# The start byte of the matmuls' moving rows: a 272-column pitch, and one that keeps every row at byte 64 of a 256-byte block

## The chip, the cores and the metric

The kernel runs on one core of a Trainium2 chip. The metric is the device time of one execution in microseconds. Names of engines: PE is TensorE, PEld its weight loads, DVE is VectorE, ACT is ScalarE, POOL is GpSimd, SP issues DMAs.

## The reference, cut to what matters

Two layers over 16 meta tokens and 256 frames (272 positions, D_MODEL 1024, D_FF 2816), all float32. Layer 0 mixes with differential attention, layer 1 with sparse attention (DSA); each layer has a feed-forward block before and after its mixer:

```python
def _swiglu(x, wi, wo):
    a, b = jnp.split(x @ wi, 2, axis=-1)
    return (jax.nn.silu(a) * b) @ wo
...
    for layer in range(DEPTH):
        h = h + 0.5 * _swiglu(_rms_norm(h, ln_ffn1[layer]), ffn1_wi[layer], ffn1_wo[layer])
        hn = _rms_norm(h, ln_mix[layer])
        ...
        h = h + mix @ w_out[layer]
        h = h + 0.5 * _swiglu(_rms_norm(h, ln_ffn2[layer]), ffn2_wi[layer], ffn2_wo[layer])
    return h[:, N_META:]
```

So there are four feed-forward blocks (FFN 1 to 4 here, the four calls of `ffn` in the code).

## The kernel before, in words

Activations lie transposed: features on the 128 partitions, positions along a row. `h` holds 8 rows (KT = 8 blocks of 128 features) of T = 272 positions. A float32 product is made of float32r parts: every operand x is split into a high part (a float32r copy) and a low part (x minus it), and `mm3` issues three matmuls for one 128x128 block of weights: high weights by high activations (L246), high weights by low activations (L247), low weights by high activations (L248). The weights are the stationary operand, and each matmul has a weight load of its own; the activations are the moving operand, streamed a row of 272 (or 256) columns at a time from the partition.

The moving rows that this document is about:

- `X["h"]` and `X["l"]`, the norms' input, split (`xh`, `xl`; 8 rows each). `prep_x` writes them after every residual add, ACT the high part and DVE the low one. They feed the first half of every FFN (the "wi" half), the attention projections and the DSA projections. For FFN 4 they lie in the tile `W` (`x2`) and are read from column 16 on, since the meta tokens are no longer needed: 256 columns.
- `ah` and `al`, the feed-forward activations, split (FT = 22 rows each), written in `evac` and `act_lo`, read in the second half of an FFN (the "wo" half).

A wi half runs over 22 weight tiles (j); in each, over k = 0 to 7, and at each k three matmuls into `pa` and three into `pb`, all six from row k of `xh` and `xl`: 48 matmuls a tile, 1,056 in all. A wo half runs over 8 output blocks, each of two weight tiles of 11 rows: 33 matmuls a tile, 528 in all. A differential attention projection takes the same 8 rows for one output after another: three matmuls at each k, 24 an output, 72 a head (queries, keys, values; 8 heads). In DSA, `cqh` and `cql` (2 rows of 256 columns each) are the moving rows of the projection `q_abs`.

Weights come by DMA from SP's queue ahead of their use (`Stream.dma`), ACT makes the high part (L116), DVE the low part (L133). All engines run their instructions in the order in which the program is written; tiles of the pools `const`, `act` and `ev` get fixed addresses, in the order of their first use.

A row of 272 float32 columns is 1088 bytes, which is 4 x 256 + 64. So where one row starts at byte 0 of a 256-byte block of its partition, the next starts at byte 64, then 128, 192, and 0 again. By the addresses in the built program:

| moving rows | first byte of the tile | row pitch, bytes | byte of rows 0, 1, 2, 3 in a 256-byte block |
|---|---|---|---|
| `xh`, `xl` (FFN 1 to 3, projections) | 27136, 35840 | 1088 | 0, 64, 128, 192 (both tiles) |
| `ah`, `al` of FFN 1 | 152512, 176448 | 1088 | 192, 0, 64, 128 and 64, 128, 192, 0 |
| `ah`, `al` of FFN 2 and 3 | 148224, 172160 | 1088 | 0, 64, 128, 192 and 128, 192, 0, 64 |
| `x2` of FFN 4, from column 16 on | 46720 | 1088 | 192, 0, 64, 128 (both parts) |
| `ah`, `al` of FFN 4, from column 16 on | 148224, 172160 | 1088 | 64, 128, 192, 0 and 192, 0, 64, 128 |
| `cqh`, `cql` | 177536, 179584 | 1024 | 128 in every row |

All weight tiles (`wh`, `wl`) start at byte 128 of such a block, and a 128-column block of weights is 512 bytes, so every weight load starts at byte 128.

The three matmuls, and the write of the split rows:

```python
        PE.matmul(ps, wh, bh, start=start, stop=False)
        PE.matmul(ps, wh, bl, start=False, stop=False)
        PE.matmul(ps, wl, bh, start=False, stop=stop)
...
        ACT.activation(xh[:, k, c], h[:, k, c], AF.Copy, scale=g(k))
        DVE.scalar_tensor_tensor(xl[:, k, c], h[:, k, c], g(k), xh.bitcast(F32)[:, k, c],
```

Of the kernel before, what the change touches and what calls it, by code (L numbers as in the profile page):

```python
# [61 lines left out]
def trunk(ctx, tc, d, out):  # L62
    nc = tc.nc
    PE, ACT, DVE, POOL = nc.tensor, nc.scalar, nc.vector, nc.gpsimd

    const = ctx.enter_context(tc.tile_pool(name="const", bufs=1))
# [6 lines left out]
    ps = ctx.enter_context(tc.tile_pool(name="ps", bufs=1, space=PSUM))  # L73

    def psa():
        return ps.tile([128, 512], F32, name="pa", bufs=3)

    def psb():
        return ps.tile([128, 512], F32, name="pb", bufs=3)

    def psc():
        return ps.tile([128, 512], F32, name="pc", bufs=2)
# [87 lines left out]
    h = const.tile([128, KT, T], F32, name="h")  # L170
# [28 lines left out]
    def ln(i):  # L199
        return lambda k: gn[:, 8 * i + k:8 * i + k + 1]  # L200

    X = dict(h=const.tile([128, KT, T], F32R, name="xh"), l=const.tile([128, KT, T], F32R, name="xl"))
    acc = const.tile([128, T], F32, name="acc")
    R = const.tile([128, T], F32, name="R")

# [3 lines left out]

    def prep_x(k, g, c0=0):  # L210
        c = slice(c0, T)
        xh, xl = X["h"], X["l"]
        ACT.activation(xh[:, k, c], h[:, k, c], AF.Copy, scale=g(k))
        DVE.scalar_tensor_tensor(xl[:, k, c], h[:, k, c], g(k), xh.bitcast(F32)[:, k, c],  # L214
                                 op0=OP.mult, op1=OP.subtract)

    def prep_s(k, c0=0):
# [20 lines left out]
    def rstd(psum_tile, c0=0):  # L238
        c = slice(c0, T)
        PE.matmul(psum_tile[:, c], ones_d, acc[:, c], start=True, stop=True)  # L240
        load = log_exp_tables()
        t = small.tile([128, T], F32, name="sq")
        rsqrt(R[:, c], psum_tile[:, c], t[:, c], load)

    def mm3(ps, wh, wl, bh, bl, start, stop):
# [6 lines left out]
    for k in range(KT):  # L252
        c = slice(256 * k, 256 * k + 256)
        prep_x(k, ln(0))
        ACT.copy(wh0[:, c], r0[:, c])  # L255
        DVE.tensor_tensor(wl0[:, c], r0[:, c], wh0.bitcast(F32)[:, c], OP.subtract)
# [9 lines left out]
    W = const.tile([128, 16, T], F32, name="W")  # L266
# [13 lines left out]
    def evac_h(mt, ps, half, g, c0):  # L280
        c = slice(c0, T)
        if half:
            DVE.scalar_tensor_tensor(h[:, mt, c], ps[:, c], 0.5, h[:, mt, c], op0=OP.mult, op1=OP.add)
        else:
            DVE.tensor_tensor(h[:, mt, c], ps[:, c], h[:, mt, c], OP.add)
        if g is None:
            nc.sync.dma_start(out[:, mt, :], h[:, mt, c])
        else:
            prep_x(mt, g, c0)
            prep_s(mt, c0)  # L290

    def ffn(g_next, c0=0, extra=None, first=0):
        c = slice(c0, T)
        with tc.tile_pool(name="act", bufs=1) as actp, tc.tile_pool(name="ev", bufs=2) as ev:
            ah = actp.tile([128, FT, T], F32R, name="ah")
            al = actp.tile([128, FT, T], F32R, name="al")
            ub = {}

            def act_lo(j):
                DVE.tensor_tensor(al[:, j, c], ub.pop(j)[:, c], ah.bitcast(F32)[:, j, c], OP.subtract)  # L300

            def evac(j, pa, pb):
                t = ev.tile([128, T], F32, name="t")
                s = ev.tile([128, T], F32, name="s")
                b = ev.tile([128, T], F32, name="b")
                DVE.tensor_tensor(t[:, c], pa[:, c], R[:, c], OP.mult)  # L306
                last_silu.append(ACT.activation(s[:, c], t[:, c], AF.Silu))
                DVE.tensor_tensor(b[:, c], pb[:, c], R[:, c], OP.mult)
                ws.ahead()
                if j:  # L310
                    act_lo(j - 1)
                DVE.tensor_tensor(b[:, c], s[:, c], b[:, c], OP.mult)  # L312
                ACT.copy(ah[:, j, c], b[:, c])  # L313
                ub[j] = b

            pairs = {}
            for j in range(FT):
                wh, wl = ws.next()
                pa, pb = psa(), psb()
                for k in range(KT):  # L320
                    for m, ps in ((0, pa), (1, pb)):
                        s = slice((2 * k + m) * 128, (2 * k + m + 1) * 128)
                        mm3(ps[:, c], wh[:, s], wl[:, s], X["h"][:, k, c], X["l"][:, k, c],
                            k == 0, k == KT - 1)
                pairs[j] = pa, pb
                if j == first:
                    rstd(psc(), c0)
                    if extra:
                        extra(psc())
                if j >= first:  # L330
                    for i in sorted(pairs):
                        evac(i, *pairs.pop(i))
            act_lo(FT - 1)

            for mt in range(KT):
                ps = psc()
                for half in range(2):
                    wh, wl = ws.next()
                    for kk in range(11):
                        f = half * 11 + kk  # L340
                        s = slice(kk * 128, kk * 128 + 128)
                        mm3(ps[:, c], wh[:, s], wl[:, s], ah[:, f, c], al[:, f, c], f == 0, f == FT - 1)
                    if half == 0:
                        ws.ahead()
                evac_h(mt, ps, True, g_next, c0)
                ws.ahead()

    def diff_attention():
        with tc.tile_pool(name="da", bufs=2) as da, tc.tile_pool(name="dp", bufs=1) as dp:
# [11 lines left out]
            for i in range(2):  # L361
                p = dp.tile([128, 400], F32, name=f"pta{i}")
# [19 lines left out]
            def proj_qk(i):  # L382
                wh, wl = ws.next()
                ps = (psc(), psc()) if i == 1 else (pj(), pj())
                for m in range(2):
                    for k in range(KT):
                        s = slice((2 * k + m) * 128, (2 * k + m + 1) * 128)
                        mm3(ps[m][:, :T], wh[:, s], wl[:, s], X["h"][:, k, :], X["l"][:, k, :], k == 0, k == KT - 1)
                    if i == 0 and m == 0:
                        rstd(ps1())  # L390
                st[i] = dict(ps=ps)
# [21 lines left out]
            def proj_v(i):  # L413
                wh, wl = ws.next()
                ps = pj()
                for k in range(KT):
                    s = slice(k * 128, k * 128 + 128)
                    mm3(ps[:, :T], wh[:, s], wl[:, s], X["h"][:, k, :], X["l"][:, k, :], k == 0, k == KT - 1)
                v = da.tile([128, T], F32, name="v")
                DVE.tensor_tensor(v, ps[:, :T], R, OP.mult)  # L420
                st[i]["v"] = v
# [32 lines left out]
            def logits(i):  # L454
# [29 lines left out]
                for m in range(2):  # L484
                    DVE.tensor_tensor(mt[:, m, :], ps[m][0:16, 416:432], W[0:16, m * AH + i, 144:160], OP.add)
                DVE.tensor_reduce(out=ms[:, 0:2], in_=mt, axis=AX.X, op=OP.max)
                DVE.tensor_tensor(mt, mt, ms[:, 0:2].unsqueeze(2).to_broadcast([16, 2, NM]), OP.subtract)
                ACT.activation(mt, mt, AF.Exp)

            def soft_fin(i):  # L490
# [93 lines left out]
            n = AH  # L584
# [7 lines left out]
            g = [pj(), pj(), None, None]  # L592
# [31 lines left out]
    def dsa():  # L624
        q0 = NM
        Q = slice(q0, T)
        with tc.tile_pool(name="sa", bufs=2) as sa, tc.tile_pool(name="sp", bufs=1) as sp, \
# [16 lines left out]
            def ps1():  # L644
                turn[0] ^= 1
                return (psa, psb)[turn[0]]()
# [58 lines left out]
            for m in range(4):  # L705
                ps = ps1()
                for k in range(2):
                    s = slice((2 * m + k) * 128, (2 * m + k + 1) * 128)
# [202 lines left out]
            n = BH  # L911
            for i in range(n):
# [14 lines left out]
                    soft_fin(i - 1)  # L927
                if i >= 3:
                    av(i - 3)
            x2 = const.tile([128, 16, T], F32R, name="W")  # L930
            X["h"], X["l"] = x2[:, 0:KT, :], x2[:, KT:16, :]

            def wout_part(ps, w, m, k0, k1):
                wh, wl = w
# [6 lines left out]
            g = [psc(), None, None, None]  # L941
# [20 lines left out]
            for grp in (2, 3):  # L962
                w = ws.next()
                for m in range(2):
                    ps = psc()
# [1 line left out]
                    evac_h(2 * grp + m, ps, False, ln(5), q0)  # L967
                ws.ahead()

    ffn(ln(1), extra=build_bias, first=1)  # L970
    diff_attention()
    once.close()
    ffn(ln(3))
    ffn(ln(4))
    dsa()
    ffn(None, c0=NM)


def _layout(inp):
# [49 lines left out]
    oh = np.zeros((32, 400), f)  # L1029
    for j in range(NREL):  # L1030
        rel = j - 271
# [22 lines left out]
```

## Time and profile before

| | |
|---|---|
| time, median of 3 runs | 1081.26 us (1081.1 to 1084.32) |
| span of the profiled execution, first to last instruction | 1079.7 us, 1.6 below the median |
| PE busy | 1067.9 us, 99% of the span |
| weight loads busy (they overlap the matmuls) | 1021.7 us, 95% |
| DVE busy | 689.6 us, 64% |
| ACT busy | 542.7 us, 50% |
| DMA queue of the weights | 46.0% of 16 engines' span |

A matmul's duration in the trace is some 280 to 290 ns, more than twice the distance from one start to the next, because matmuls are pipelined. So busy time is no measure of what one costs; the distance between starts is. It is read from the timeline, whose starts have two decimals (10 ns), by dividing a stretch by the number of matmuls in it.

### The profile page before, as it was taken

What the parts mean: (1) busy time and instruction counts of PE and PEld (TensorE: products, weight loads), DVE (VectorE), ACT (ScalarE), POOL (GpSimd) and SP (SyncE); (2) the same over time, 40 slices, a digit from 0 to 9 for tenths busy, and PEclk for the clock granted to TensorE, in tenths of its full rate; (3) what the DMA queues carried; (4) which work ended last, traced back from release to release, by engine and by line L of the source; (5) the groups of instructions that cost most, each with busy time, mean ns of one, the idle gap of its engine ahead of it and who ended that gap; (6) DMA issues with size and microseconds to landing.
All of it is one profiled execution on the core that took longest, in us unless ns stands there. A gap on an engine that the chain in (4) does not pass through costs nothing.

```text
span 1079.7 us, 20010 instructions
## 1 busy us (share of the span) xinstructions
PE 1067.9 (99%) x8332; PEld 1021.7 (95%) x8332; DVE 689.6 (64%) x1191; ACT 542.7 (50%) x876; POOL 77.2 (7%) x111
## 2 busy tenths in 40 slices
PE   8999999999999999999999999999999999999998
PEld 7999999998889999999999999999876799999998
DVE  6567645577777666655576666546898657666542
ACT  6455444356687544444454444535856545444331
POOL 1200000042210000000000000000153100000000
PEclk9999999999999999999999999999999999999999
DMA  8985445533343454445654544455422025554461
GB/s 295 210 233 204 151 154 169 190 134 128 128 153 117 166 187 168 172 129 170 213 204 164 188 161 142 161 172 201 156 91 90 1 101 181 189 195 171 147 200 68
DMA packets 30809, 174.20 MB, mean 161 GB/s; under 512 B 3664, under 2 KB 5216, under 8 KB 16896
## 3 DMA queue, kind: packets, MB, share of 16 engines
q1 hardware_dynamic: 29808, 169.99, 46.0%
q0 software_dynamic: 912, 2.95, 1.5%
q8 instruction: 65, 1.06, 0.4%
q14 instruction: 24, 0.20, 0.1%
HBM read 171.47 MB, written 1.46 MB: 160 GB/s over the span
## 4 chain that ended last, share of the span: by engine, by line
PE 92%; DMA 2%; DVE 2%; ACT 1%; issue 1%; POOL 0%; SPq 0%; DVEq 0%; POOLq 0%; ACTq 0%
PE pa L246 11%; PE pa L247 11%; PE pa L248 11%; PE pc L246 9%; PE pc L247 9%; PE pc L248 9%; PE pb L247 8%; PE pb L246 8%; PE pb L248 8%; DMA wr<-w_ffn_wi 2%; PE pc L858 1%; PE pc L861 1%; DVE wl L133 1%; DMA h<-hT 1%; DVE sel L794 1%
## 5 line engine op out<-in xcount | busy, mean ns | idle before, releaser
L116 ACT CAST wh<-wr 128x2048 fp32r<-128x2048 f32 (+3 forms) x180 | 301.0, 1673 | 347.5 <-PE pb L247 176.0
L133 DVE TENSOR_TENSOR wl<-wr,wh 128x2048 fp32r<-128x2048 f32 (+3 forms) x188 | 368.0, 1958 | 48.6 <-PE pc L248 29.4
L246 PE MATMUL pa<-xh,wh 128*128 128x272 f32 (+1 forms) x736 | 213.0, 290 | 2.4 <-ACT wh L255 2.4
L248 PE MATMUL pa<-xh,wl 128*128 128x272 f32 (+1 forms) x736 | 212.7, 289 | 1.5 <-DVE wl L133 1.5
L247 PE MATMUL pa<-xl,wh 128*128 128x272 f32 (+1 forms) x736 | 213.1, 290 | 0.0
L246 PE MATMUL pc<-ah,wh 128*128 128x272 f32 (+1 forms) x704 | 201.6, 286 | 0.0
L247 PE MATMUL pc<-al,wh 128*128 128x272 f32 (+1 forms) x704 | 201.2, 286 | 0.0
L248 PE MATMUL pc<-ah,wl 128*128 128x272 f32 (+1 forms) x704 | 200.9, 285 | 0.0
L247 PE MATMUL pb<-xl,wh 128*128 128x272 f32 (+1 forms) x544 | 157.4, 289 | 0.0
L248 PE MATMUL pb<-xh,wl 128*128 128x272 f32 (+1 forms) x544 | 156.8, 288 | 0.0
L246 PE MATMUL pb<-xh,wh 128*128 128x272 f32 (+1 forms) x544 | 156.0, 287 | 0.0
L246 PEld LDWEIGHTS pa<-xh,wh 128*128 128x128 f32 x736 | 139.0, 189 | 7.3 <-ACT wh L255 3.7
L248 PEld LDWEIGHTS pa<-xh,wl 128*128 128x128 f32 x736 | 138.6, 188 | 2.0 <-DVE wl L133 1.7
L247 PEld LDWEIGHTS pa<-xl,wh 128*128 128x128 f32 x736 | 138.5, 188 | 0.2
L247 PEld LDWEIGHTS pc<-al,wh 128*128 128x128 f32 x704 | 132.6, 188 | 0.0
L248 PEld LDWEIGHTS pc<-ah,wl 128*128 128x128 f32 x704 | 132.5, 188 | 0.0
L246 PEld LDWEIGHTS pc<-ah,wh 128*128 128x128 f32 x704 | 132.3, 188 | 0.0
L306 DVE TENSOR_TENSOR t<-pa,R 128x272 f32<-128x272 f32 (+1 forms) x88 | 38.4, 436 | 117.0 <-PE pa L248 116.6
L246 PEld LDWEIGHTS pb<-xh,wh 128*128 128x128 f32 x544 | 103.1, 189 | 0.0
L247 PEld LDWEIGHTS pb<-xl,wh 128*128 128x128 f32 x544 | 102.5, 188 | 0.2 <-DVE xl L214 0.2
L248 PEld LDWEIGHTS pb<-xh,wl 128*128 128x128 f32 x544 | 102.4, 188 | 0.0
L313 ACT CAST ah<-b 128x272 fp32r<-128x272 f32 (+1 forms) x88 | 36.6, 416 | 75.1 <-DVE b L312 75.1
(326 smaller groups left out, 1723.9 us busy)
## 6 DMA issues: line engine op xcount, KB each, us to landing
wr<-w_ffn_wi SPq DMA_DIRECT2D x85, 1024.0 KB, 4.8
wr<-w_ffn_wo SPq DMA_DIRECT2D x64, 704.0 KB, 4.1
wr<-w_qk SPq DMA_DIRECT2D x8, 1024.0 KB, 4.7
wr<-w_out SPq DMA_DIRECT2D x8, 1024.0 KB, 4.9
wr<-w_v SPq DMA_DIRECT2D x8, 512.0 KB, 3.3
wr<-w_uqa SPq DMA_DIRECT2D x4, 1024.0 KB, 4.8
W<-fd POOLq DMA_DIRECT2D x8, 272.0 KB, 18.9
wr<-w_ffn_wi SPq DMA_DIRECT2D x7, 256.0 KB, 6.5
```

The costliest lines, as they stand in the source:

```text
L116: ACT.copy(w[:, c], self.raw[i][:, c])
L133: DVE.tensor_tensor(w[:, c], r[:, c], self.h[i].bitcast(F32)[:, c], OP.subtract)
L246: PE.matmul(ps, wh, bh, start=start, stop=False)
L247: PE.matmul(ps, wh, bl, start=False, stop=False)
L248: PE.matmul(ps, wl, bh, start=False, stop=stop)
L306: DVE.tensor_tensor(t[:, c], pa[:, c], R[:, c], OP.mult)
L313: ACT.copy(ah[:, j, c], b[:, c])
L794: DVE.scalar_tensor_tensor(sel[:, b, kc], r[:, kc], wt[:, b, 2 * i + e:2 * i + e + 1], sel[:, b, kc], op0=OP.mult, op1=OP.add)
L858: PE.matmul(ps[:, B1], qas[i][:, 256 * k + 128:256 * k + 256], ckg[:, k, :], start=k == 0, stop=k == 1)
L861: PE.matmul(ps[:, B0], qas[i][:, 256 * k:256 * k + 128], ckg[:, k, 0:144], start=k == 0, stop=k == 1)
```

## The change

The rows get a pitch of a whole number of 256-byte blocks, and padding ahead of the tiles puts the first one at byte 64. `xh` and `xl` get rows of 320 columns (1280 bytes, XS), `ah` and `al` rows of 320 columns in FFN 1 to 3 and of 256 in FFN 4 (AS). In FFN 4 the activations are written from column 0 of their rows, no longer from column 16, and so is `x2`, which becomes 17 x 256 columns, addressed 48 columns in. The columns that are computed are the same.

```diff
+XS = 320
+AS = (320, 320, 320, 256)
...
-    X = dict(h=const.tile([128, KT, T], F32R, name="xh"), l=const.tile([128, KT, T], F32R, name="xl"))
+    const.tile([128, 16], F32, name="pad0")
+    X = dict(h=const.tile([128, KT, XS], F32R, name="xh"), l=const.tile([128, KT, XS], F32R, name="xl"), o=0)
+    const.tile([128, 48], F32, name="pad1")
...
-        xh, xl = X["h"], X["l"]
-        ACT.activation(xh[:, k, c], h[:, k, c], AF.Copy, scale=g(k))
-        DVE.scalar_tensor_tensor(xl[:, k, c], h[:, k, c], g(k), xh.bitcast(F32)[:, k, c],
+        xh, xl, xc = X["h"], X["l"], slice(c0 - X["o"], T - X["o"])
+        ACT.activation(xh[:, k, xc], h[:, k, c], AF.Copy, scale=g(k))
+        DVE.scalar_tensor_tensor(xl[:, k, xc], h[:, k, c], g(k), xh.bitcast(F32)[:, k, xc],
...
-    def ffn(g_next, c0=0, extra=None, first=0):
+    def ffn(i, g_next, c0=0, extra=None, first=0):
         c = slice(c0, T)
+        ac = slice(0, T - c0)
+        xc = slice(c0 - X["o"], T - X["o"])
...
-            ah = actp.tile([128, FT, T], F32R, name="ah")
-            al = actp.tile([128, FT, T], F32R, name="al")
+            actp.tile([128, 32 if i == 0 else 16], F32, name="pad2")
+            ah = actp.tile([128, FT, AS[i]], F32R, name="ah")
+            al = actp.tile([128, FT, AS[i]], F32R, name="al")
...
-                        mm3(ps[:, c], wh[:, s], wl[:, s], X["h"][:, k, c], X["l"][:, k, c],
+                        mm3(ps[:, c], wh[:, s], wl[:, s], X["h"][:, k, xc], X["l"][:, k, xc],
...
-                        mm3(ps[:, c], wh[:, s], wl[:, s], ah[:, f, c], al[:, f, c], f == 0, f == FT - 1)
+                        mm3(ps[:, c], wh[:, s], wl[:, s], ah[:, f, ac], al[:, f, ac], f == 0, f == FT - 1)
...
-                        mm3(ps[m][:, :T], wh[:, s], wl[:, s], X["h"][:, k, :], X["l"][:, k, :], k == 0, k == KT - 1)
+                        mm3(ps[m][:, :T], wh[:, s], wl[:, s], X["h"][:, k, 0:T], X["l"][:, k, 0:T], k == 0, k == KT - 1)
...
-            x2 = const.tile([128, 16, T], F32R, name="W")
-            X["h"], X["l"] = x2[:, 0:KT, :], x2[:, KT:16, :]
+            x2 = const.tile([128, 17, SEQ], F32R, name="W").rearrange("p k t -> p (k t)")
+            n2 = KT * SEQ
+            X["h"] = x2[:, 48:n2 + 48].rearrange("p (k t) -> p k t", t=SEQ)
+            X["l"] = x2[:, n2 + 48:2 * n2 + 48].rearrange("p (k t) -> p k t", t=SEQ)
+            X["o"] = NM
```

By the addresses in the built program, every row of `xh`, `xl`, `x2`, `ah` and `al` then starts at byte 64 of a 256-byte block, in all four FFNs. DSA's first projection reads `xh` and `xl` from column 16 on, which is byte 128 in every row. `cqh`, `cql` and the weight tiles stay at byte 128. Attention's output rows (`oh`, `ol`) and DSA's (`o_h`, `o_l`) keep their pitch of 272 columns.

## Rows read from the trace of the kernel before

**Rows 1.** The profile's page: span, busy time of the engines, the chain.
```profile
span 1079.7 us, 20010 instructions
...
PE 1067.9 (99%) x8332; PEld 1021.7 (95%) x8332; DVE 689.6 (64%) x1191; ACT 542.7 (50%) x876; POOL 77.2 (7%) x111
...
PE 92%; DMA 2%; DVE 2%; ACT 1%; issue 1%; POOL 0%; SPq 0%; DVEq 0%; POOLq 0%; ACTq 0%
```

**Rows 2.** Busy time in two stretches, FFN 2's and FFN 4's first halves.
```profile
core 0: us, PE busy (x) PEld busy (x) DVE busy (x) ACT busy (x) POOL busy (x), PEclk, DMA share, GB/s
360.80:480.80 120.00, 120.00 (x963) 120.00 (x961) 75.68 (x103) 51.93 (x61) 0.00 (x0) 1.00 0.47 163
901.60:1013.90 112.30, 112.30 (x963) 112.30 (x962) 74.22 (x103) 51.37 (x61) 0.00 (x0) 1.00 0.50 175
```

**Rows 3.** Timeline, PE: first matmuls of halves, the last matmul of FFN 4.
```profile
360.80 0.29 PE L246 MATMUL pa<-xh,wh 128*128 128x272 f32 x1
...
480.80 0.29 PE L246 MATMUL pc<-ah,wh 128*128 128x272 f32 x1
...
546.77 0.29 PE L246 MATMUL pa<-xh,wh 128*128 128x272 f32 x1
...
901.61 0.28 PE L246 MATMUL pa<-W,wh 128*128 128x256 f32 x1
...
1013.88 0.28 PE L246 MATMUL pc<-ah,wh 128*128 128x256 f32 x1
...
1076.03 0.28 PE L248 MATMUL pc<-ah,wl 128*128 128x256 f32 x1
```

**Rows 4.** Timeline, PE: two float32 matmuls of 272 columns, and what follows.
```profile
820.65 0.62 PE L858 MATMUL pc<-ckg,qa 128*128 128x272 f32 x2
821.11 0.27 PE L883 MATMUL pb<-cst,p 128*128 128x128 f32 x1
```

**Rows 5.** Timeline, PE: group starts in one wi tile of FFN 3.
```profile
607.24 0.29 PE L246 MATMUL pa<-xh,wh 128*128 128x272 f32 x1
...
608.00 0.28 PE L246 MATMUL pa<-xh,wh 128*128 128x272 f32 x1
...
608.37 0.28 PE L246 MATMUL pb<-xh,wh 128*128 128x272 f32 x1
...
608.74 0.28 PE L246 MATMUL pa<-xh,wh 128*128 128x272 f32 x1
...
609.49 0.28 PE L246 MATMUL pa<-xh,wh 128*128 128x272 f32 x1
...
610.24 0.29 PE L246 MATMUL pa<-xh,wh 128*128 128x272 f32 x1
```

**Rows 6.** Timeline, PE: group starts in one wi tile of FFN 4.
```profile
912.84 0.28 PE L246 MATMUL pa<-W,wh 128*128 128x256 f32 x1
...
914.25 0.28 PE L246 MATMUL pa<-W,wh 128*128 128x256 f32 x1
...
914.60 0.28 PE L246 MATMUL pb<-W,wh 128*128 128x256 f32 x1
...
914.94 0.28 PE L246 MATMUL pa<-W,wh 128*128 128x256 f32 x1
...
915.64 0.28 PE L246 MATMUL pa<-W,wh 128*128 128x256 f32 x1
```

**Rows 7.** Timeline, PE: 24 matmuls whose rows all start at byte 128, first and last.
```profile
785.05 0.28 PE L246 MATMUL pb<-cqh,wh 128*128 128x256 f32 x1
...
787.81 0.28 PE L248 MATMUL pb<-cqh,wl 128*128 128x256 f32 x1
```

**Rows 8.** Timeline, PE: start of k = 1 and of k = 5 in one attention projection.
```profile
260.19 0.29 PE L246 MATMUL pa<-xh,wh 128*128 128x272 f32 x1
...
261.70 0.29 PE L246 MATMUL pa<-xh,wh 128*128 128x272 f32 x1
```

**Rows 9.** The page's groups: one form of weight load, mean ns behind the comma.
```profile
L246 PEld LDWEIGHTS pa<-xh,wh 128*128 128x128 f32 x736 | 139.0, 189 | 7.3 <-ACT wh L255 3.7
```

More of the change, by code (lines that the diff above doesn't have):

```diff
@@ L290, in evac_h @@
             prep_s(mt, c0)
-    def ffn(g_next, c0=0, extra=None, first=0):
+    def ffn(i, g_next, c0=0, extra=None, first=0):
         c = slice(c0, T)
+        ac = slice(0, T - c0)
+        xc = slice(c0 - X["o"], T - X["o"])
         with tc.tile_pool(name="act", bufs=1) as actp, tc.tile_pool(name="ev", bufs=2) as ev:
-            ah = actp.tile([128, FT, T], F32R, name="ah")
-            al = actp.tile([128, FT, T], F32R, name="al")
+            actp.tile([128, 32 if i == 0 else 16], F32, name="pad2")
+            ah = actp.tile([128, FT, AS[i]], F32R, name="ah")
+            al = actp.tile([128, FT, AS[i]], F32R, name="al")
             ub = {}
             def act_lo(j):
-                DVE.tensor_tensor(al[:, j, c], ub.pop(j)[:, c], ah.bitcast(F32)[:, j, c], OP.subtract)
+                DVE.tensor_tensor(al[:, j, ac], ub.pop(j)[:, c], ah.bitcast(F32)[:, j, ac], OP.subtract)
             def evac(j, pa, pb):
@@ L312, in evac @@
                 DVE.tensor_tensor(b[:, c], s[:, c], b[:, c], OP.mult)
-                ACT.copy(ah[:, j, c], b[:, c])
+                ACT.copy(ah[:, j, ac], b[:, c])
                 ub[j] = b
@@ L330, in ffn @@
                 if j >= first:
-                    for i in sorted(pairs):
-                        evac(i, *pairs.pop(i))
+                    for n in sorted(pairs):
+                        evac(n, *pairs.pop(n))
             act_lo(FT - 1)
@@ L417, in proj_v @@
                     s = slice(k * 128, k * 128 + 128)
-                    mm3(ps[:, :T], wh[:, s], wl[:, s], X["h"][:, k, :], X["l"][:, k, :], k == 0, k == KT - 1)
+                    mm3(ps[:, :T], wh[:, s], wl[:, s], X["h"][:, k, 0:T], X["l"][:, k, 0:T], k == 0, k == KT - 1)
                 v = da.tile([128, T], F32, name="v")
@@ L968, in dsa @@
                 ws.ahead()
-    ffn(ln(1), extra=build_bias, first=1)
+    ffn(0, ln(1), extra=build_bias, first=1)
     diff_attention()
     once.close()
-    ffn(ln(3))
-    ffn(ln(4))
+    ffn(1, ln(3))
+    ffn(2, ln(4))
     dsa()
-    ffn(None, c0=NM)
+    ffn(3, None, c0=NM)
 def _layout(inp):
```

## The prediction

> **What bounds the kernel now.** I read the page's first lines and its chain, then the matmuls' start times stage by stage, then single weight tiles.
>
> TensorE (PE) is the bound. It is busy 1067.9 of the 1079.7 us span, and 92% of the chain that ended last is PE [rows 1]. In the feed-forward (FFN) stages it never stands still: in 120.00 us of the second FFN's first half PE is busy 120.00, while DVE is busy 75.68, ACT 51.93 and the DMA engines 0.47 of the time; the fourth FFN's first half reads 112.30, 74.22, 51.37 and 0.50 [rows 2]. [...] What sets the end is therefore the gap from one matmul's start to the next, times the number of matmuls; a nanosecond on each of 5,000 is 5 us.
>
> From start times and counts (48 matmuls per wi tile, 33 per wo tile) [rows 3]: the second FFN's wi half runs 20 tiles from 360.80 to 480.80, 120.00 us / 960 = 125.0 ns a matmul; its wo half 65.97 / 528 = 124.9; the fourth FFN's wi half (256 columns) 112.27 / 960 = 116.9; its wo half, first to last start, 62.15 / 527 = 117.9.
>
> [...]
>
> [...] With a pitch of 1088 bytes, rows k, k+1, k+2, k+3 start at bytes 0, 64, 128, 192 of a 256-byte block. One wi tile of the third FFN starts its six-matmul groups for k = 4 to 7 at 607.24, 608.00, 608.74, 609.49, and the next begins at 610.24 [rows 5]: 0.76, 0.74, 0.75, 0.75 us, and the shortest is the one at byte 64. The fourth FFN shows it better. Two groups at bytes 192 and 0 take 1.41 us (912.84 to 914.25: 117.5 ns a matmul), the group at byte 64 takes 0.69, the one at byte 128 0.70 [rows 6]. Within the byte-64 group it settles: the first three take 0.35, the last three 0.34 (914.60 to 914.94: 113.3 ns).
>
> A run in which all rows share one byte exists already. The low-rank projection's input cqh and cql has 1024-byte rows, all at byte 128. It repeats one gap: 785.05 to 787.81 over 23 gaps is 120.0 ns [rows 7], dearer than the mixed 116.9. So the byte matters, the gap has a memory of a few matmuls, and a uniform layout locks to a value of its own, which may be better or worse than the mixture.
>
> **The change part by part.** No instruction is added, removed or moved: the built programs list the same 8,040 PE rows, and those of the other engines, in the same order. No DMA changes size or target. What changes is the byte at which the moving operand's row starts.
>
> 1. FFN 1 to 3, both halves: 3 x (1,056 + 528) = 4,752 matmuls of 272 columns go from mixed bytes to byte 64. Now 125.0 ns. No run of 272 columns at one byte is longer than six, so the new gap is bounded. [...] Above: the uniform run at byte 128 sits 3 ns over its mixture, which would make 128. Nearest row: the last three of the byte-64 group, 608.37 to 608.74, 0.37 / 3 = 123.3 [rows 5]. I take that, since at 256 columns the last three are the settled value. 4,752 x (125.0 - 123.3) = 8.1 us.
> 2. Differential attention's projections, 8 x 72 = 576 matmuls of 272 columns: here one output's eight rows follow each other, three matmuls at each byte, at 1.51 us / 12 = 126 ns (260.19 to 261.70) [rows 8]. To 123.3: 1.6 us. The 72 of the DSA stage's other projections at the same price: 0.2 us.
> 3. Fourth FFN, wi: 1,056 matmuls to byte 64, 116.9 to 113.3 ns [rows 3, 6]: 3.8 us. Its wo half, 528 matmuls, 117.9 to 113.3: 2.4 us.
> 4. DSA's first projection reads 256 columns from the seventeenth on, so its 48 matmuls go to byte 128 throughout, the case of the uniform run [rows 7]: 48 x (120 - 117) = 0.1 us lost.
> 5. Padding tiles and larger buffers: no instruction, so no engine time. Buffers that now lie over others of an earlier stage can only add waits at a stage's start. The second FFN's first t lies where attention's oh was, whose last reader is a PE matmul ahead of the FFN's own, and t waits for those anyway: nothing. The converted weights must keep up with a faster PE: a wi tile would take 48 x 113.3 = 5.44 us where DVE works 74.22 / 20 = 3.7 and ACT 2.6 on it [rows 2]. If that cover went, the gap would be DVE's 3.7 us a tile, still shorter.
>
> Sum: 8.1 + 1.6 + 0.2 + 3.8 + 2.4 - 0.1 = 16.0 us. The profiled span of 1079.7 stands 1.6 below the median of 1081.26, so 1063.7 in the span and about **1065** as measured.
>
> [...] Each matmul has a weight load that lasts 189 ns [rows 9], longer than the gap, so loads run under the streams all the time, and every weight block starts at byte 128. I suspect these two readers of meeting in the same part of a partition; the trace doesn't name the partner. [...]
>
> **The rivals.**
> - *272 columns lock low.* If all 5,400 settle between 119 and 121.5 ns, for which the 256-column group speaks and the 0.74 us group does not, step 1 gives 17 to 28 us, step 2 some 3 to 4, and the time is 1042 to 1056. Chance 0.18.
> - *272 columns gain nothing* (124.6 to 126 ns): unlike at 256 columns, the group at byte 64 settles nowhere, its first three matmuls take 0.37 us and its last three 0.37 [rows 5], and its lead over the others is 1 to 3 ns a matmul. Then the fourth FFN's 6.1 us and at most 3 more remain, or up to 5 are lost: 1072 to 1080. Chance 0.15.
> - *A bad lock.* A uniform byte loses what the mixture averages, as byte 128 shows at 256 columns. 272 columns are 1088 bytes, so each row ends in the 64-byte piece in which the next begins, unlike 256 columns. If 4,752 + 72 matmuls settle at 128 ns and 576 lose 2, that is 14.5 + 1.2 us against the 6.1 gained: 1091. It decides from 126.3 ns on, where 1.3 x 4,752 = 6.2 us eats the gain. Chance 0.06.
> - *Nothing happens.* The six-matmul pattern comes from the order of PSUM tiles and lines, not from the byte; the same byte does have different gaps within a group. Then 1081. Against it: the uniform run at byte 128 gives one gap on all its lines [rows 7]. Chance 0.09. [...]
>
> **How the numbers follow.** The forecast (121.5 to 124.6 ns at 272 columns, 1056 to 1072) has 0.52, and 1065 is its value by rows. Below 1045 lies little, above 1079 the last two rivals and the tail of the second, so the range 1045 to 1079 leaves out about 0.2. 0.3% of 1081 is 3.2 us, about what a measurement of this kernel tells from no change. Faster than 1078.0: 0.52 + 0.18 + 0.12 of the second rival = 0.82. Within: 0.03 + 0.09 = 0.12. Slower: 0.06.
>
> **What the changed profile would show.** Right: every matmul of a wi tile with the same gap, tiles of the second FFN starting every 5.92 us instead of 6.00, of the fourth every 5.44 instead of 5.61, wo halves of 65.1 and 59.8 us, the same busy times on DVE and ACT. Wrong: gaps that still alternate (the byte is not the cause), tiles of 6.06 us or more (a bad lock), or PE idle time at stage starts where there was none.

## The result, and the profile after

The changed kernel takes 1067.88 us (median of 4 runs, 1066.17 to 1069.46) against 1081.18 of before on the same chip (4 runs): ratio 0.9857, 95% interval 0.9836 to 0.9878, 13.3 us less. Timed once more later, the ratio was 0.9877 (0.9857 to 0.9898). The forecast was 1065.

The page of the profiled execution (1066.74 us), to be read against [rows 1]:

```profile
span 1064.9 us, 20010 instructions
...
PE 1052.2 (99%) x8332; PEld 1006.5 (95%) x8332; DVE 689.1 (65%) x1191; ACT 543.1 (51%) x876; POOL 77.2 (7%) x111
```

PE's busy time fell by 15.7 us; DVE and ACT do what they did. The kernel is as much bound by PE as before.

The two stretches of [rows 2], as the 20 tiles now lie (same columns: PE, PEld, DVE, ACT, POOL, granted clock, DMA share, GB/s):

```profile
357.41:475.81 118.40, 118.40 (x963) 118.40 (x961) 75.51 (x103) 51.92 (x61) 0.00 (x0) 1.00 0.48 166
892.72:1001.52 108.80, 108.80 (x962) 108.80 (x961) 73.83 (x103) 51.41 (x61) 0.00 (x0) 1.00 0.52 181
```

The same work on DVE and ACT, the same clock, but 118.40 us where it was 120.00, and 108.80 where it was 112.30 (112.27 between matmul starts). The rows that answer to [rows 3], PE's timeline (start, duration, operation; the three matmuls of `mm3` are L250 to L252 now):

```profile
357.41 0.28 PE L250 MATMUL pa<-xh,wh 128*128 128x272 f32 x1
...
475.81 0.28 PE L250 MATMUL pc<-ah,wh 128*128 128x272 f32 x1
...
540.93 0.28 PE L250 MATMUL pa<-xh,wh 128*128 128x272 f32 x1
...
892.72 0.28 PE L250 MATMUL pa<-W,wh 128*128 128x256 f32 x1
...
1001.52 0.28 PE L250 MATMUL pc<-ah,wh 128*128 128x256 f32 x1
...
1061.25 0.28 PE L252 MATMUL pc<-ah,wl 128*128 128x256 f32 x1
```

118.40 / 960 = 123.33 ns a matmul (it was 125.0), the wo half 65.12 / 528 = 123.33 (124.9), the fourth FFN 108.80 / 960 = 113.33 (116.9) and 59.73 / 527 = 113.34 (117.9).

And the gap is now one gap. A wi tile of FFN 3, its groups of six, beside [rows 5]:

```profile
606.51 0.28 PE L250 MATMUL pa<-xh,wh 128*128 128x272 f32 x1
...
607.25 0.28 PE L250 MATMUL pa<-xh,wh 128*128 128x272 f32 x1
...
608.00 0.28 PE L250 MATMUL pa<-xh,wh 128*128 128x272 f32 x1
...
612.43 0.28 PE L250 MATMUL pa<-xh,wh 128*128 128x272 f32 x1
```

0.74 or 0.75 for each group, and 5.92 for the tile, which is 8 x 0.74: what only the byte-64 group took before is now the rule. The attention projection of [rows 8] likewise, from k = 1 to k = 5:

```profile
257.65 0.29 PE L250 MATMUL pa<-xh,wh 128*128 128x272 f32 x1
...
259.13 0.29 PE L250 MATMUL pa<-xh,wh 128*128 128x272 f32 x1
```

1.48 / 12 = 123.3 ns, where it was 126.

Where the time came from, by comparing when the same matmul starts in the two traces:

| stage | forecast, us | measured, us |
|---|---|---|
| up to 23 us | 0 | -1.1 |
| rest of FFN 1 | 2.7 | 3.1 |
| attention | 1.6 | 1.2 |
| FFN 2 and 3 | 5.4 | 5.2 |
| DSA | 0.1 | 0.2 |
| FFN 4 | 6.2 | 6.2 |
| sum | 16.0 | 14.8 |

The one entry of another sign is the start. PE's wait there for the first tile's conversion, and the stretch in which the clock fell (waits: us in total, times, longest; then the columns of [rows 2]):

```profile
PE pa L250 <- ACT wh L259: 3.7, 2, 2.7
...
10.00:15.00 5.00, 4.48 (x23) 4.48 (x24) 4.45 (x12) 4.82 (x14) 0.00 (x0) 0.66 1.05 387
```

PE waited up to 2.7 us (1.9 in the profile of before) for ACT's high part of a tile, and after that wait the granted clock read 0.50 from 11 to 14 us, where matmuls start 0.23 us apart, and 1.00 again from 14.5 us on, where they start 0.13 apart: 0.66 on the mean of the stretch, where before has 1.00. Whether that belongs to the change is taken up in experiment 5.

### The profile page after: what moved, and what is told of

Same layout as the page of the kernel before. It is cut to its first block, busy times and chain, and to the rows that moved or that the text cites. A ratio compares the mean times of both kernels' runs of the same rounds, so it can differ in the third digit from the quotient of the medians.

```text
span 1064.9 us, 20010 instructions
## 1 busy us (share of the span) xinstructions
PE 1052.2 (99%) x8332; PEld 1006.5 (95%) x8332; DVE 689.1 (65%) x1191; ACT 543.1 (51%) x876; POOL 77.2 (7%) x111
## 4 chain that ended last, share of the span: by engine, by line
PE 90%; DMA 3%; DVE 3%; ACT 2%; issue 1%; POOL 0%; SPq 0%; DVEq 0%; ACTq 0%; POOLq 0%
PE pa L250 10%; PE pa L251 10%; PE pa L252 10%; PE pc L250 9%; PE pc L251 9%; PE pc L252 9%; PE pb L250 8%; PE pb L252 8%; PE pb L251 8%; DMA wr<-w_ffn_wi 3%; PE pc L865 1%; DVE wl L135 1%; ACT wh L118 1%; PE pc L868 1%; DVE sel L801 1%
## 5 line engine op out<-in xcount | busy, mean ns | idle before, releaser
L135 DVE TENSOR_TENSOR wl<-wr,wh 128x2048 fp32r<-128x2048 f32 (+3 forms) x188 | 368.0, 1958 | 45.6 <-PE pc L252 28.0
L250 PE MATMUL pa<-xh,wh 128*128 128x272 f32 (+1 forms) x736 | 213.3, 290 | 3.8 <-ACT wh L259 3.7
L252 PE MATMUL pa<-xh,wl 128*128 128x272 f32 (+1 forms) x736 | 211.1, 287 | 0.9 <-DVE wl L135 0.9
L250 PE MATMUL pc<-ah,wh 128*128 128x272 f32 (+1 forms) x704 | 199.8, 284 | 0.0
L252 PE MATMUL pc<-ah,wl 128*128 128x272 f32 (+1 forms) x704 | 199.8, 284 | 0.0
L252 PE MATMUL pb<-xh,wl 128*128 128x272 f32 (+1 forms) x544 | 156.5, 288 | 0.0
L250 PE MATMUL pb<-xh,wh 128*128 128x272 f32 (+1 forms) x544 | 156.4, 288 | 0.0
L250 PEld LDWEIGHTS pa<-xh,wh 128*128 128x128 f32 x736 | 138.8, 189 | 8.3 <-ACT wh L259 4.9
L252 PEld LDWEIGHTS pa<-xh,wl 128*128 128x128 f32 x736 | 138.9, 189 | 1.2 <-DVE wl L135 1.2
L252 PEld LDWEIGHTS pc<-ah,wl 128*128 128x128 f32 x704 | 132.5, 188 | 0.0
L250 PEld LDWEIGHTS pc<-ah,wh 128*128 128x128 f32 x704 | 132.5, 188 | 0.0
L252 PEld LDWEIGHTS pb<-xh,wl 128*128 128x128 f32 x544 | 103.0, 189 | 0.0
L250 PEld LDWEIGHTS pb<-xh,wh 128*128 128x128 f32 x544 | 102.9, 189 | 0.0
```

The lines of the kernel that those rows point to most:

```text
L135: DVE.tensor_tensor(w[:, c], r[:, c], self.h[i].bitcast(F32)[:, c], OP.subtract)
```

## The experiments

Theories at the start. **A**: the gap follows the distance between the moving row's byte and the weights' byte in the circle of 256, because two readers meet. **B**: the row's own byte counts. **C**: any uniform byte would do, since alternation itself costs. Below, "wi" and "wo" are an FFN's two halves; each gap is a stretch of starts divided by its matmuls, and all diffs are against the changed kernel. The runs of before on these chips read 1080.4 to 1087.2 us, so single runs are compared by gaps and spans.

### 1. Only `ah` and `al` at byte 64

```diff
-XS = 320
+XS = 272
...
-            x2 = const.tile([128, 17, SEQ], F32R, name="W").rearrange("p k t -> p (k t)")
...
+            x2 = const.tile([128, 16, T], F32R, name="W")
```

> One part of the change alone: ah and al at byte 64, while xh, xl and x2 keep the pitch of 272 columns. If the parts add up, the wo halves are those of the changed kernel (123.3 and 113.3 ns) and the wi halves those of before (125.0 and 117.0): 1,584 x 1.7 + 528 x 4.5 ns = 5.0 us less than before, about 1076. If a half's gap depends on how the half before it left the matmuls and loads standing to each other, a wo half may settle at another value than 123.3.

Measured: 1076.49 us, span 1074.7. PE's timeline, start and end of FFN 4's wi half (20 tiles) and the last recorded start but one of its wo half:

```profile
898.99 0.28 PE L248 MATMUL pa<-W,wh 128*128 128x256 f32 x1
...
1011.26 0.28 PE L248 MATMUL pc<-ah,wh 128*128 128x256 f32 x1
...
1070.89 0.28 PE L249 MATMUL pc<-al,wh 128*128 128x256 f32 x1
```

112.27 / 960 = 116.9 ns in the half left alone, as in [rows 3], and 59.63 / 526 = 113.4 in the half at byte 64. At 272 columns 125.0 and 123.34. The parts add: the gain is local to the matmuls whose rows moved.

### 2. Other bytes, as uniform

```diff
-    const.tile([128, 16], F32, name="pad0")
...
-            actp.tile([128, 32 if i == 0 else 16], F32, name="pad2")
+            actp.tile([128, (48, 48, 56, 64)[i]], F32, name="pad2")
...
-            X["h"] = x2[:, 48:n2 + 48].rearrange("p (k t) -> p k t", t=SEQ)
+            X["h"] = x2[:, 16:n2 + 16].rearrange("p (k t) -> p k t", t=SEQ)
```

Rows of X at byte 0 (192 in FFN 4); `ah` and `al` at 128, 192, 224, 0.

> As the changed kernel, but the rows of xh and xl start at byte 0, ah and al at byte 128 (FFN 1), 192 (FFN 2) and 224 (FFN 3), x2 at byte 192, ah and al of FFN 4 at byte 0; each uniform. Theory 'byte': each byte has a gap of its own, and 64 is the cheapest of those in the kernel before: by the six-matmul groups there, wi halves at byte 0 settle at about 126 ns, wo at 128 and 192 at about 125, FFN 4's wi at 192 at 117.5 and its wo at 0 at about 117; together with the projections some 14 to 20 us more than the changed kernel, 1081 to 1088. Rival 'uniform': it is the mixture that costs and any one byte serves; then every 272-column half stays at 123.3 and the 256-column ones at 113.3, and the time at 1068.

Measured: 1095.09 us, span 1093.3. FFN 2's and FFN 4's wi halves:

```profile
368.03 0.29 PE L248 MATMUL pa<-xh,wh 128*128 128x272 f32 x1
...
489.63 0.29 PE L248 MATMUL pc<-ah,wh 128*128 128x272 f32 x1
...
914.03 0.28 PE L248 MATMUL pa<-W,wh 128*128 128x256 f32 x1
...
1027.09 0.28 PE L248 MATMUL pc<-ah,wh 128*128 128x256 f32 x1
```

121.60 / 960 = 126.67 ns at byte 0, 113.06 / 960 = 117.8 at byte 192: uniform rows at a poor byte are dearer than the mixture of before (125.0 and 116.9). Theory C falls. This is what the rival "a bad lock" describes, at other bytes than 64. The time lies above the 1081 to 1088 that were expected: the gaps came out 0.3 to 1.7 ns above those read from the mixture's groups (byte 192 at 272 columns most, 126.66 for 125), and the kernel before took 1086.66 us beside this run.

A second kernel of this kind puts X at byte 96, `ah` and `al` at 32, 160, 0 and 32 (the same lines, other numbers):

> As the changed kernel, but xh and xl at byte 96, ah and al at byte 32 (FFN 1), 160 (FFN 2) and 0 (FFN 3), x2 at byte 96, ah and al of FFN 4 at byte 32. Theory 'byte': a gap of its own for each, no two need be alike; rows at byte 0 in a wo half give the same gap as rows at byte 0 in the wi halves of the run with bytes 0, 128, 192, 224. A byte between two 64-byte pieces may be better than 123.3 or 113.3 or worse; nothing here tells. Rival 'uniform': 123.3 and 113.3 throughout, 1068.

Measured: 1086.94 us, span 1085.2. FFN 1's last 12 wi tiles, then FFN 2's 20, both at byte 96:

```profile
75.00 0.29 PE L250 MATMUL pa<-xh,wh 128*128 128x272 f32 x1
...
147.96 0.29 PE L250 MATMUL pc<-ah,wh 128*128 128x272 f32 x1
...
363.02 0.29 PE L250 MATMUL pa<-xh,wh 128*128 128x272 f32 x1
...
483.35 0.29 PE L250 MATMUL pc<-ah,wh 128*128 128x272 f32 x1
```

72.96 / 576 = 126.67 ns and 120.33 / 960 = 125.34, from the same rows and the same byte. In FFN 1 the gap was 125.33 too, until a wait of PE between the tiles at 67 and 75 us (an estimate of it: these start 8 us apart, and 48 x 125.33 ns is 6.0, so some 2 us). So one byte can have two steady gaps, and here the change came with a break in the stream. None of the theories has that. Byte 0 in a wo half reads 126.66, as it did in the wi halves of the first kernel.

A third kernel tries finer steps: `ah` and `al` at 48, 80, 40 and (FFN 4) 80, X at 64 (80 in FFN 4):

```diff
-AS = (320, 320, 320, 256)
+AS = (320, 320, 320, 320)
+OFF = (4, 4, 2, 4)
...
-            ah = actp.tile([128, FT, AS[i]], F32R, name="ah")
+            ah = actp.tile([128, FT, AS[i]], F32R, name="ah")[:, :, OFF[i]:]
```

> As the changed kernel, but ah and al start between the 32-byte steps: byte 48 in FFN 1, 80 in FFN 2, 40 in FFN 3, 80 in FFN 4; x2 at byte 80. xh and xl stay at 64. Theory 'pieces of 64 bytes' (a row that starts inside a piece touches one piece more): every one of these is dearer than 64, by 1 ns or more, at 272 and at 256 columns. Rival: 64 is not the best byte, and one of the neighbours gives less than 123.3 or 113.3.

Measured: 1079.87 us, span 1078.1. FFN 4's wi half at byte 80:

```profile
897.17 0.28 PE L251 MATMUL pa<-W,wh 128*128 128x256 f32 x1
...
1011.57 0.28 PE L251 MATMUL pc<-ah,wh 128*128 128x256 f32 x1
```

114.40 / 960 = 119.17 ns, against 113.33 sixteen bytes below. At 272 columns bytes 40 and 48 give 123.37 and 123.35, as good as 64, and byte 80 gives 126.66. So the expectation that each of them is dearer by 1 ns or more, since a row that starts inside a 64-byte piece touches one piece more, fails at 40 and 48. No byte tried beats 64.

### 3. The weights' byte

Weights at byte 192, X at 128, `ah` and `al` at 64, 128, 192 and 64:

```diff
-    const.tile([128, 16], F32, name="pad0")
+    const.tile([128, 32], F32, name="pad0")
...
+    const.tile([128, 16], F32, name="pad3")
...
-            actp.tile([128, 32 if i == 0 else 16], F32, name="pad2")
+            actp.tile([128, (16, 16, 32, 64)[i]], F32, name="pad2")
```

> All weight tiles are moved from byte 128 to byte 192, and the moving rows lie: xh, xl at 128; ah, al at 64 (FFN 1), 128 (FFN 2), 192 (FFN 3); x2 at 128; ah, al of FFN 4 at 64; cqh, cql at 192. Theory 'two readers' (the gap depends on the distance between the moving row's byte and the weights' byte): the wi halves and FFN 2's wo stay at 123.3, FFN 4's wi at 113.3, q_abs at 120; FFN 1's wo and FFN 4's wo change to what byte 0 gives beside weights at 128, FFN 3's wo to what byte 128 gives. Rival 'row byte alone': FFN 4's wi goes to 120.0 (byte 128), q_abs to about 117.5 (byte 192), FFN 1's wo stays at 123.3 and FFN 4's wo at 113.3.

Measured: 1083.11 us, span 1081.3. FFN 2's and FFN 3's wi halves, 20 tiles each, and FFN 4's wo half from first to last start:

```profile
362.09 0.28 PE L250 MATMUL pa<-xh,wh 128*128 128x272 f32 x1
...
480.49 0.28 PE L250 MATMUL pc<-ah,wh 128*128 128x272 f32 x1
...
558.07 0.29 PE L250 MATMUL pa<-xh,wh 128*128 128x272 f32 x1
...
679.67 0.29 PE L250 MATMUL pc<-ah,wh 128*128 128x272 f32 x1
...
1015.10 0.28 PE L250 MATMUL pc<-ah,wh 128*128 128x256 f32 x1
...
1077.64 0.28 PE L252 MATMUL pc<-ah,wl 128*128 128x256 f32 x1
```

118.40 / 960 = 123.33, as 64 beside 128. But 121.60 / 960 = 126.67 in the next FFN, from the same rows at the same bytes, and 117.78 in FFN 4's wi half. Row byte 64 beside weights at 192 reads 126.66 (wo of FFN 1), as byte 0 beside 128, and 62.54 / 527 = 118.67 in FFN 4, where byte 0 beside 128 read 118.65 and byte 64 beside 128 reads 113.33; 192 beside 192 reads 125.34, as 128 beside 128. So six of the eight halves speak for the distance, and two show a second gap again.

The same kernel once more:

> The kernel with the weights at byte 192 and most moving rows at byte 128 once more, unaltered. If a stall draws one of two steady gaps by chance, the wi halves at byte 128 come out in another assortment than 123.3, 123.3, 126.7 (272 columns) and 117.8 (256 columns). If something fixed in the program decides it (where the stage starts, which weight buffer comes first), the same halves show the same gaps to 0.1 ns.

Measured: 1084.08 us; the same halves with the same gaps (123.33, 123.33, 126.67, 117.78). So in these two executions, on two chips, the gaps were not drawn anew; this speaks for something fixed in the program, as far as one repeat can.

Weights at byte 0 and all FFN rows at byte 192:

> All weights at byte 0, all moving rows of the feed-forward halves at byte 192: 64 bytes behind the weights' byte in the circle of 256, as 64 is beside 128. If only the distance between the two counts, 123.3 ns at 272 columns and 113.3 at 256 return in every half, and the span is that of the changed kernel, 1064 to 1067. If the row's own byte counts, 126.7 and 117.8, as byte 192 gave beside weights at 128: about 19 us more. If the distance only offers two steady gaps and a stall draws one, some halves read the one and some the other.

```diff
-    const.tile([128, 16], F32, name="pad0")
+    const.tile([128, 48], F32, name="pad0")
...
+    const.tile([128, 32], F32, name="pad3")
```

Measured: 1070.77 us, span 1069.0. FFN 3's and FFN 4's wi halves:

```profile
557.23 0.29 PE L250 MATMUL pa<-xh,wh 128*128 128x272 f32 x1
...
675.63 0.29 PE L250 MATMUL pc<-ah,wh 128*128 128x272 f32 x1
...
896.78 0.28 PE L250 MATMUL pa<-W,wh 128*128 128x256 f32 x1
...
1005.58 0.28 PE L250 MATMUL pc<-ah,wh 128*128 128x256 f32 x1
```

118.40 / 960 = 123.33 and 108.80 / 960 = 113.33, in all eight halves. Byte 192 was dear beside weights at 128 (126.66 and 117.8) and is the best here. Theory B falls: the weights' byte is a partner. One caution: 126.67 and 117.78 are also the dear ones of the two gaps seen at the distance of -64, so by themselves these values leave open that byte 192 has such a pair of its own, whatever the weights' byte. The three values that byte 192 has at 272 columns (126.66, 125.34 and 123.33 beside weights at 128, 192 and 0) and byte 64's 118.67 beside weights at 192, which is neither 113.33 nor 117.78, are what B can't give.

Last, the whole pattern shifted by 64 bytes, weights at 192 and all rows at 128:

> All weights at byte 192 and all moving rows of the feed-forward halves at byte 128: the changed kernel moved by 64 bytes as a whole, weights and rows together. If only the distance counts, 123.3 and 113.3 ns in every half, the third FFN's and the fourth's first halves too, and the time of the changed kernel (1066 to 1070 us). Then the 126.7 and 117.8 ns that these two halves showed with the weights at byte 192 came from what the other halves' rows had set before them. If the program's place, and not the bytes before, decides between two steady gaps, the third FFN's first half reads 126.7 and the fourth's 117.8 once more, and the time is about 3.5 + 4.9 = 8.4 us above, 1075 to 1078.

```diff
-    const.tile([128, 16], F32, name="pad0")
+    const.tile([128, 32], F32, name="pad0")
...
+    const.tile([128, 16], F32, name="pad3")
```

Measured: 1081.49 us (10 runs, 1079.72 to 1084.93), ratio to before 0.9987 (0.997 to 1.0004). The whole gain is gone at an unchanged distance, so theory A alone isn't enough either. PE's timeline around FFN 3's first tile, its other tiles, and the same in FFN 4 (L244 is the norm's statistic, a float32 matmul, two instructions in the trace, that stands between the first and the second wi tile):

```profile
543.73 0.28 PE L250 MATMUL pa<-xh,wh 128*128 128x272 f32 x1
...
549.65 0.62 PE L244 MATMUL pc<-acc,ones_d 128*128 128x272 f32 x2
...
556.19 0.29 PE L250 MATMUL pa<-xh,wh 128*128 128x272 f32 x1
...
677.79 0.29 PE L250 MATMUL pc<-ah,wh 128*128 128x272 f32 x1
...
893.44 0.28 PE L250 MATMUL pa<-W,wh 128*128 128x256 f32 x1
...
894.12 0.28 PE L250 MATMUL pa<-W,wh 128*128 128x256 f32 x1
...
894.80 0.59 PE L244 MATMUL pc<-acc,ones_d 128*128 128x256 f32 x2
...
900.88 0.28 PE L250 MATMUL pa<-W,wh 128*128 128x256 f32 x1
...
1013.95 0.28 PE L250 MATMUL pc<-ah,wh 128*128 128x256 f32 x1
```

FFN 3's first tile runs at 5.92 / 48 = 123.3 ns. The statistic breaks the stream: the next matmul starts 0.26 us behind it (549.91), and the one after that another 0.33 later (550.24). The 20 tiles behind the second tile run at 121.60 / 960 = 126.67; the dear gap begins with the first matmuls behind the statistic. In FFN 4 six matmuls ahead of the statistic take 0.68 (113.3), the 20 tiles behind it 113.07 / 960 = 117.8. Both wo halves, which follow without a break, keep the dear gap (126.67, 117.78). FFN 1 and 2 pass the same kind of break and stay at 123.33. Of the two expectations the second is met: FFN 3's and FFN 4's wi halves are the dear ones again, although the other halves' rows now lie elsewhere. The time is above its 1075 to 1078, because the wo halves behind them are dear too. The dear halves cost 3.2 + 1.8 + 4.3 + 2.3 = 11.6 us, which is the 12.1 between this span (1079.7) and the 1067.6 of experiment 5, within half a us.

### 4. Does a shorter weight load free the stream?

If the load's reads are what the stream meets, less load should cost less. In FFN 2 and 4 the second of the three wo matmuls uses only half of its weight columns:

```diff
+    def mm3h(ps, wh, wl, bh, bl, start, stop):
...
+        PE.matmul(ps[0:64], wh[:, 0:64], bl, start=False, stop=False)
...
```

> As the changed kernel, but in the wo halves of FFN 2 and FFN 4 the second matmul of each three uses only the first 64 of its 128 weight columns, so the weight load that runs while the first matmul streams is half as long; the upper half of that product is left out. [...] Rival 'row byte alone' (pieces of a partition that a stream crosses): no gap changes.

Measured: span 1065.4. The loads (mean ns of one behind the comma) and FFN 4's wo half:

```profile
L256 PEld LDWEIGHTS pc<-al,wh 128*64 128x64 f32 x352 | 47.3, 134 | 0.0
...
1001.97 0.28 PE L255 MATMUL pc<-ah,wh 128*128 128x256 f32 x1
...
1061.58 0.28 PE L256 MATMUL pc<-al,wh 128*64 128x256 f32 x1
```

A third of the loads take 134 ns instead of 188 (not the half that was expected), and the gap stays 59.61 / 526 = 113.33; FFN 2's rose to 123.70. If the two met, the shorter load should have lowered the gap; neither half shows a fall.

Shorter still, in all three matmuls of a block and all FFNs (only the first and last blocks of an output load in full):

```diff
+        w0, w1 = ((0, 32), (16, 128), (0, 64), (0, 32))[i]
+        p = slice(0, 128) if start or stop else slice(0, w1 - w0)
+        w = slice(0, 128) if start or stop else slice(w0, w1)
```

> As the changed kernel, but in the wo halves all matmuls of rows 1 to 20 (of 22) use part of their weight columns, so their loads are shorter: FFN 1 and FFN 4 the first 32 of 128, FFN 3 the first 64, FFN 2 columns 16 to 127, so that the load starts 64 bytes later, at byte 192. Most of the output's upper part is left out. Theory 'overlap' (a load in progress delays the stream): halves with 32-column loads fall to 116 to 118 ns (FFN 1) and 109 to 111 (FFN 4), FFN 3 somewhat less, FFN 2 stays near 123.3. Theory 'start' (what counts is where the load begins relative to the row, not how long it is): FFN 1 and 3 stay at 123.3, FFN 4 at 113.3, as with half a load in one of three, and FFN 2 goes to the 126.7 that rows at byte 64 gave beside weights at byte 192.

Measured: span 1071.0. FFN 1's wo half, whose loads are of 32 columns:

```profile
L258 PEld LDWEIGHTS pc<-ah,wh 128*32 128x32 f32 x320 | 34.6, 108 | 3.4
...
148.08 0.28 PE L258 MATMUL pc<-ah,wh 128*128 128x272 f32 x1
...
213.82 0.29 PE L260 MATMUL pc<-ah,wl 128*128 128x272 f32 x1
```

108 ns a load, yet 65.74 / 527 = 124.7 ns a matmul, more than with full loads; FFN 2 to 4 read 124.34, 124.39 and 113.33. So at the cheap distance a shorter load gives nothing back, and the theory "overlap" misses in every half with loads of 32 or 64 columns. That a load in progress delays the stream at a dear distance isn't ruled out: the cheap distance may be the one at which the two don't meet at all, and the only shortened loads at a dear one, FFN 2's, were shortened little (174 ns) and moved their start as well. Whether it is the load's start that counts is not shown either: FFN 1 and 3 did not stay at 123.3, and FFN 2's loads start at byte 192 there and gave 124.34, not the 126.7 of that distance.

Last of these, high and low part at different bytes: `ah` at 64 and `al` at 128, 192, 0 and (FFN 4) 128:

```diff
+            actp.tile([128, (16, 32, 48, 16)[i]], F32, name="pad4")
```

> As the changed kernel, but al (the low parts) starts at another byte than ah (64): 128 in FFN 1 and FFN 4, 192 in FFN 2, 0 in FFN 3. Theory 'byte': a matmul's gap follows its own row's byte, so the wo halves' mean is that of two rows at 64 and one at the other byte: (2 x 123.3 + 125.3) / 3 = 124.0 in FFN 1, 124.4 in FFN 2 and FFN 3, (2 x 113.3 + 120) / 3 = 115.6 in FFN 4. Rival 'whole cycle' (the three matmuls lock together, and only their sum has a steady value): a sum that these means do not give, above or below.

Measured: span 1073.1. FFN 4's wo half:

```profile
1006.59 0.28 PE L250 MATMUL pc<-ah,wh 128*128 128x256 f32 x1
...
1069.31 0.28 PE L251 MATMUL pc<-al,wh 128*128 128x256 f32 x1
```

62.72 / 526 = 119.24 ns (by the exact starts 119.26), dearer than the mean of the uniform gaps of byte 64 (two of three matmuls, 113.3) and byte 128 (one of three, 120.0 [rows 7]), which is 115.6. At 272 columns 124.45 to 124.48, close to the mean. At 256 columns, then, the gap of one matmul depends on its neighbours' bytes as well as its own, unless byte 128 has a second gap of some 131 ns, which no run shows.

### 5. The changed kernel again

> The changed kernel once more (moving rows at byte 64, weights at byte 128), timed in five rounds. If the byte alone fixes the gap, every half shows 123.3 and 113.3 ns again, and the time is 1066 to 1068 in every round but for the start-up. If the same bytes have two steady gaps and each stall or new half draws one, a 272-column half somewhere reads 126.7 (1,056 x 3.3 ns = 3.5 us) or a 256-column half 117.8 (4.7 us), and the times come in steps of that size; the two groups among its four times so far (about 1066.5 and 1069.3) would be such a step.

Measured: 1069.42 us (5 runs, 1067.82 to 1071.82), before 1083.22 (9 runs, 1080.82 to 1085.24), ratio 0.9877. In this profile, span 1067.6, all halves show 123.33 and 113.33 again, to 0.01 ns; no half took the other gap. Yet the end lies 2.7 us behind that of the first profile, and FFN 1's end already does (211.65 against 208.93). Two stretches in FFN 1, columns as in [rows 2]:

```profile
50.00:60.00 10.00, 8.87 (x68) 8.24 (x66) 5.28 (x9) 2.66 (x3) 0.00 (x0) 1.00 1.06 201
60.00:65.00 5.00, 3.48 (x21) 3.48 (x22) 1.47 (x1) 1.88 (x2) 0.00 (x0) 0.80 0.94 299
```

PE is idle for 2.65 us there, waiting for the low part of a weight tile (DVE, L135), and the clock reads 0.80 behind the first of the gaps; the first profile has none of it in these 15 us. Before's runs on this chip spread by 4.4 us, after's by 4.0. So these two profiled executions differ in FFN 1, where PE waits for weights, and not by a step of 3.5 or 4.7 us; no change of gap was seen between them. Of the other executions only times are known, and four of these five lie above the expected 1066 to 1068.

## Why the prediction was right

The mechanism holds as far as it went, and so does nearly every size. Beside weights that stay at byte 128 the gap follows the moving row's byte (at 272 columns 125.34 ns at byte 128 and 126.67 at byte 0); a uniform row at byte 64 settles at 123.33 ns at 272 columns (123.3 forecast) and 113.33 at 256 (113.3). Two parts of this were luck. The 123.3 was read from starts to 10 ns: 0.37 / 3 stands for 120 to 127. To the nanosecond, and over FFN 3's 20 tiles of the kernel before, the last three gaps of the byte-64 group are 123, 124 and 122, on the mean 123.0, so nothing had settled there; at 256 columns they are 113.4, 113.3 and 113.4, and that value was well read. And the "memory of a few matmuls" is one of a thousand and more: at this distance there is a second steady gap (126.67 and 117.78 ns, experiment 3), and that the changed kernel fell into the cheaper one nothing in the prediction's rows could tell. By the steps of the sum:

- Step 1 (8.1 us): 3.1 + 5.2 = 8.3. Some 0.5 of it is no gap: from 50 to 75 us PE was idle for 0.94 us, before 1.47.
- Step 2 (1.6 + 0.2): the gap came out as forecast (123.3); 1.2 us arrived in the attention stage, where PE is idle for 0.30 of 136.17 us (before 0.21 of 137.33). Where the rest of the missing 0.4 us went was not separated.
- Step 3 (6.2): 6.2.
- Step 4 (-0.1): DSA as a whole gained 0.2 where 0.1 was forecast.
- Step 5 (nothing): holds in the FFNs; DVE and ACT kept up with the faster PE (75.51 and 51.92 us busy in the 118.40 us of FFN 2's 20 tiles, and PE never idle).
- Not in the sum: 1.1 us lost before 23 us. The second profile of the same kernel lost 0.3 there and more between 50 and 65 us, so this varies with the run. Whether the change has a price in FFN 1 is open: the stages behind 23 us gain 15.9 us between the two profiles, but the medians lie only 13.3 and 13.8 us apart, and the second interval (0.9857 to 0.9898, 11.0 to 15.5 us) leaves 15.9 out. The conversion to the median assumed 1.6 us between span and median; the four runs' median stands 3.0 above this profile's span.

The rival "272 columns lock low" (119 to 121.5 ns, where the 256-column gap by its columns, 113.3 x 272 / 256 = 120.4, would lie) did not occur at any byte: 123.33 is the lowest steady gap seen. "272 columns gain nothing" did not occur at this distance. "Nothing happens" falls by the result and by experiments 2 and 3, where the order of PSUM tiles and lines is the same and the gap changes with the byte. "A bad lock" is real: 126.67 ns in experiments 2 and 3, and in the last kernel of experiment 3 it ate the whole gain, at the distance that the changed kernel uses. What spared this change is not understood well enough to forecast it for another layout.

Of the suspected cause, the meeting of stream and weight load, half is shown: the weights' byte matters as well as the row's (row byte 192 at 272 columns gave 126.66, 125.34 and 123.33 ns beside weights at 128, 192 and 0, experiment 3). That the two meet, and where, is not shown. Experiment 4 speaks against it as far as a load of 108 instead of 188 ns gave nothing back at the cheap distance (113.33 ns at 256 columns as with full loads, 124.7 at 272). **Open**: whether and where in the machine the two meet, and what decides between two steady gaps after a break. No experiment moved a break alone.

Steady gaps in ns by the distance (row's byte minus weights' byte; two values where both were seen):

| distance | 272 columns | 256 columns |
|---|---|---|
| -96 (32 beside 128) | 123.34 | 117.34 |
| -88 (40 beside 128) | 123.37 | not tried |
| -80 (48 beside 128) | 123.35 | not tried |
| -64 (64 beside 128; 192 beside 0) | 123.33; 123.33 | 113.33; 113.33 |
| -64 (128 beside 192) | 123.33 or 126.67 | 113.3 or 117.78 |
| -48 (80 beside 128) | 126.66 | 119.17 |
| -32 (96 beside 128) | 125.33 or 126.67 | 118.33 |
| 0 (128 beside 128; 192 beside 192) | 125.34; 125.34 | 120.0 [rows 7] |
| 32 (160 beside 128) | 125.71 | not tried |
| 64 (192 beside 128) | 126.66 | 117.78 |
| 96 (224 beside 128) | 126.66 | not tried |
| 128 (0 beside 128; 64 beside 192) | 126.67; 126.66 | 118.65; 118.67 |

## What to carry to other kernels

Where PE is the bound and never idle, look at the distances between starts per row, not at busy times: the mixed pitch here showed in its own groups which byte was cheap (six matmuls in 0.69 us at byte 64, 0.70 at byte 128 [rows 6]). The end of the cheap group gave the new gap at 256 columns, where its gaps had become equal; at 272 columns they had not, and the hit was in part luck. Place moving rows and weights together, since neither byte alone fixed the gap here (experiment 3), and look at the gap of every half afterwards: behind a break in the stream it rose to 126.67 ns, from 123.3 behind a statistic (experiment 3) and from 125.33 behind a wait (experiment 2), and the next hundreds of matmuls ran at it. Gains of this kind are to be measured for each layout; a shift of everything by 64 bytes lost this one (1081.49 us, ratio 0.9987).

## What the runs showed of the hardware that was not expected

- Two steady gaps at the same bytes: 123.33 and 126.67 ns (272 columns), 113.3 and 117.78 (256), 125.33 and 126.67 at another distance. Where the gap changed at unchanged bytes, it changed behind a break of the stream, and it then held for hundreds of matmuls, 1,488 in FFN 3 of the last kernel of experiment 3. Two profiled executions of one program fell into the same gaps, twice.
- Small shifts, large steps: at 256 columns byte 64 gives 113.33 and byte 80 gives 119.17 beside the same weights. At 272 columns 32, 40, 48 and 64 give the same 123.3 to 123.4, and 80 gives 126.66.
- Four of the gaps, taken over one, two or three matmuls, come out as multiples of 6.67 ns: 113.33 = 17 x 6.67, 126.67 = 19 x 6.67, 2 x 123.33 = 37 x 6.67, 3 x 117.78 = 53 x 6.67. Others of the table do so only over more (4 x 118.33 = 71 x 6.67, 5 x 125.33 = 94 x 6.67). Why was not examined.
- Weight loads of 108, 134 or 188 ns left the gap at 256 columns and the cheap distance at 113.33; at 272 columns shorter loads went with gaps of 123.70 to 124.7.
